# Neighbourhood attention on one Trainium2 core: the scores of two heads in one PSUM tile of two banks

## The chip, the core and the metric

One core of a Trainium2 chip runs the whole program in one launch. The metric is the device time of one execution in microseconds (us). Three executions of the kernel before took 3437.06, 3450.85 and 3451.09 us, a median of 3450.85 us.

## The reference, cut to what matters

The program is two networks in a row: a block with two attention layers and a mixture of experts, and then a two-layer block whose layers mix tokens in three ways at once (gated linear attention, a short convolution, neighbourhood attention) and end in a feed-forward part with a convolution. All arithmetic is in float32. The change sits in the neighbourhood attention of the second block. It has 512 tokens on a grid of 8 rows and 64 columns, six heads of 64 columns each, and 256 context tokens; each token attends to a window of 8 rows and 16 columns with a learnt bias, and to the whole context, under one softmax:

```python
def neighbourhood_attention(q, k, v, k_ctx, v_ctx, rpb):
    ...
    qg = grid(q.astype(jnp.float32) * (NA_DH ** -0.5))
    ...
        s_loc = jnp.einsum('bqhd,bikhd->bhqik', q_r, k_band) + jnp.transpose(bias, (0, 2, 1, 3))[None]
        s_loc = jnp.where(col_mask[None, None, :, None, :], s_loc, NEG_INF)
        s_ctx = jnp.einsum('bqhd,bchd->bhqc', q_r, kc)
        s = jnp.concatenate([s_loc.reshape(bsz, NA_HEADS, GRID_W, kh * GRID_W), s_ctx], axis=-1)
        p = jax.nn.softmax(s, axis=-1)
        ...
        o = jnp.einsum('bhqik,bikhd->bqhd', p_loc, v_band) + jnp.einsum('bhqc,bchd->bqhd', p_ctx, vc)
```

The last line adds the products of the probabilities with the values of the window and of the context.

## The kernel before, in words

The second block's main part ("latent", `lat` in the code) starts when the mixture of experts is done. It runs two layers; each is a mixer (`mixing`, line 1137) and a feed-forward part (`ffn`, line 1696). `whole` (line 1800) opens one PSUM pool, `pp`, for all of it, with four tags of two banks each: `mm`, `sc`, `tp` and `po`, which are the eight banks of PSUM. `bank` (line 163) takes a tile of one bank from it by tag. In `ffn` two more names are mapped onto the same tags: `ua` onto `mm` and `ub` onto `sc`.

In a mixer the tag `sc` is used by the gated linear attention (lines 1545, 1630 and 1688) and then by the neighbourhood attention `na` (line 1433). `na` handles the 512 queries in four blocks `b` of 128 (16 grid columns of 8 rows). For each block it loads the bias rows by DMA, adds the column mask on GpSimd (line 1450) and then goes through three pairs `j` of heads: 12 pairs in a layer, 24 in all. For one pair:

- two `sc` tiles of one bank are taken, one for each head (line 1454). Head 0 of a pair (`par` 0) has its queries and keys on partitions 0 to 63, head 1 on 64 to 127. Two matmuls for each head write its scores: 248 columns of the window (line 1460) and 256 of the context (line 1462). They are traced in the order window of both heads, context of both heads. A float32 matmul shows as two records in the trace.
- for each head VectorE adds the bias to the window's scores and takes their maximum in one instruction (line 1473), takes the context's maximum (line 1475) and joins the two (line 1476). ScalarE takes both exponentials (lines 1477 and 1478); the second reads the scores' bank last, and after it the bank is free. The sum and its reciprocal are VectorE's (lines 1479 and 1480); GpSimd scales the window's probabilities (line 1481) and VectorE the context's (line 1482).
- `pv_pair` (line 1416) transposes the probabilities on TensorE in blocks of 128 (line 1425, tag `tp`), copies them out, head 0 by VectorE and head 1 by ScalarE (line 1427), and multiplies by the values (line 1430, tag `po`). There are four such blocks for each head where `b` is 0 or 3, and five where it is 1 or 2.
- `put` splits the result into two rounded parts (`split`, lines 227 and 228) for the output projection (`add_gated`, line 1248, tag `mm`).

No order is written out by hand here: the compiler's list scheduler orders each engine's instructions ahead of time, by the order in which they were traced and by when a modelled run has their inputs and their tile's slot ready. Each engine then runs its list in that order. So instructions of one pair mix with those of the pairs before it, with the short convolution (`in_conv`), which is traced beside `na`, and with the first matmuls of the output projection, which need only the parts that are finished.

Of the kernel before, what the change touches and what calls it, by code (L numbers as in the profile page):

```python
# [11 lines left out]
F32 = mybir.dt.float32  # L12
# [7 lines left out]
PSUM = bass.MemoryType.PSUM  # L20
# [109 lines left out]
class Net:  # L130
    def __init__(self, nc, tc, ins, ctx):
        self.nc, self.tc, self.ins = nc, tc, ins
        self.side, self.banks = "left", {}
        self.cst = {}
        self.load_consts(self.pool(ctx, "consts", 1), 0)
        self.ident = self.c("ident")
        self.hp = self.pool(ctx, "hp", 1)
        self.wp = self.pool(ctx, "wp", 3)
        self.dp = self.pool(ctx, "dp", 1, space=bass.MemoryType.DRAM)
# [22 lines left out]

    def bank(self, tag, shape=(128, 512)):
        tag, bufs = self.banks.get(tag, (tag, 2))
        return self.pp.tile(list(shape), F32, name=tag, tag=tag, bufs=bufs)

    def load_consts(self, pool, g):
        self.cst[g] = pool.tile([128, CONST_N[g]], F32, name=f"cst{g}")
# [968 lines left out]
    def mixing(self, l, st, xs=None, src=None, dst=None):  # L1137


        self = copy.copy(self)  # L1140
        ins = self.ins
        lat = st == 0
        last = not lat and dst is None
        T = 512 if lat else 256
        w_in, w_out = ins["w_in_2"][l], ins["w_out_2"][l]
        es = ExitStack()
        if not lat:
            self.psum(es)
            cp = self.pool(es, "cat", 1)
        with ExitStack() as e1:  # L1150
            self.sp = self.pool(e1, "sp", 2, side="right")
            self.load_columns(self.sp, l)
            if not lat:
                self.mixer_pools(e1, l, lat)
            with ExitStack() as e2:
                xp = self.pool(e2, "xTp", 1, side="right")
                self.lp = self.pool(e2, "lp", 2, side="right")
                if lat:
                    xT = self.modulated(xp, xs, st, 0, T)
                    cp = self.pool(es, "cat", 1)  # L1160
                    self.whp = self.pool(es, "whp", 4)
                    self.mixer_pools(e1, l, lat)
                else:
                    with ExitStack() as e3:
                        xT = self.modulated(xp, self.rows_in(e3, src), st, 0, T)
                    self.wp = self.pool(e2, "bw", 2)
                    self.whp = self.pool(e2, "whp", 2)
                if lat:
                    self.parts = [cp.tile([128, 4, 8, 128], F32R, name=f"cat{a}") for a in "hl"]
                elif not last:  # L1170
                    self.parts = cp.tile([128, 8, T], F32, name="cat")
                    self.cat = self.parts.rearrange("p k (t i) -> p k t i", i=128)
                heads = self.in_heads(l, w_in, xT, T, lat, last)
                if lat:
                    finished(heads)
                else:
                    yield from heads
                gla = self.gla(l, T, lat, last)
                attention = self.in_attention(w_in, xT, T, lat, last)
                if lat:  # L1180
                    rest = itertools.chain(attention, self.in_gate(w_in, xT, T, lat))
                    together(gla, rest)
                    finished(rest)
                    self.gate()
                    rest = self.in_conv(w_in, xT, T, lat)
                    together(self.na(l), rest)
                    finished(rest)
                else:
                    yield from gla
                    yield from attention  # L1190
                    if not last:
                        yield from self.in_gate(w_in, xT, T, lat)
                        self.gate()
                        yield from self.in_conv(w_in, xT, T, lat)
            if not lat:
                if not last:
                    with ExitStack() as e2:
                        self.lp = self.pool(e2, "lp", 2)
                        yield from self.ctx_attention(T)
                for o, a in ((0, self.sfin), (192, self.nkT), (960, self.nv)):  # L1200
                    n = a.shape[1] * a.shape[2]
                    self.dma(self.ctx_out[l][:, o:o + n].rearrange("p (a b) -> p a b", a=a.shape[1]), a)
        if last:
            es.close()
            return
        if lat:
            return self.add_gated(es, self.reload, w_out, l, st)
        xs = self.rows_in(es, src)
        self.wp = self.pool(es, "bw", 2)
        self.whp = self.pool(es, "whp", 2)  # L1210
        self.lp = self.pool(es, "lp", 1)
        yield from self.add_gated(es, lambda t: xs[t], w_out, l, st, dst)
# [220 lines left out]
    def na(self, l):  # L1433
# [3 lines left out]
        for b in range(4):  # L1437
# [13 lines left out]
            for j in range(3):  # L1451
                po = self.bank("po", [128, 128])
                pms = g6("npm", [128, 2, 640])
                scs = [self.bank("sc") for _ in range(2)]
                for c in range(2):
                    for par, sc in enumerate(scs):
                        rows = slice(64 * par, 64 * par + 64)
                        q = self.nqT[rows, j, 128 * b:128 * b + 128]
                        if c == 0:
                            nc.tensor.matmul(sc[:, :248], q, self.nkT[rows, j, 8 * lo:8 * lo + 248], start=True, stop=True)  # L1460
                        else:
                            nc.tensor.matmul(sc[:, 248:504], q, self.kcT[rows, j], start=True, stop=True)  # L1462
                for par, sc in enumerate(scs):
                    pm = pms[:, par]
                    mx = self.sp.tile([128, 2], F32, name="nmx")
                    den = self.sp.tile([128, 2], F32, name="nden")
                    nm, r = self.sp.tile([128, 1], F32, name="nnm"), self.sp.tile([128, 1], F32, name="nr")
                    if o:
                        nc.gpsimd.memset(pm[:, :o], 0.0)
                    if o + 248 < 128 * ntile:  # L1470
                        nc.gpsimd.memset(pm[:, o + 248:128 * ntile], 0.0)
                    win, ctxs = pm[:, o:o + 248], pm[:, 384:640]
                    V.tensor_tensor_reduce(win, sc[:, :248], bias[:, 2 * j + par].rearrange("p c r -> p (c r)"), 1.0, NEG,
                                           ALU.add, ALU.max, accum_out=mx[:, 0:1])
                    V.tensor_reduce(mx[:, 1:2], sc[:, 248:504], axis=AX.X, op=ALU.max)
                    V.tensor_scalar(nm, mx[:, 0:1], mx[:, 1:2], -1.0, op0=ALU.max, op1=ALU.mult)
                    nc.scalar.activation(win, win, AF.Exp, bias=nm, accum_out=den[:, 0:1])
                    nc.scalar.activation(ctxs, sc[:, 248:504], AF.Exp, bias=nm, accum_out=den[:, 1:2])
                    V.tensor_tensor(r, den[:, 0:1], den[:, 1:2], op=ALU.add)
                    V.reciprocal(r, r)  # L1480
                    nc.gpsimd.tensor_scalar(win, win, r, None, op0=ALU.mult)
                    V.tensor_scalar(ctxs, ctxs, r, None, op0=ALU.mult)

                def v(i, par):
                    hv = slice(128 * j + 64 * par, 128 * j + 64 * par + 64)
                    return self.nv[:, base + i, hv] if i < ntile else self.cv[:, i - ntile, hv]

                self.pv_pair([pms[:, 0], pms[:, 1]], [128 * i for i in range(ntile)] + [384, 512], v, po)
                yield int(j % 2 == 1 or b == 3)
                self.put(lambda a: a[:, 5 + j].rearrange("p t (r c) -> p c t r", c=64)[:, 16 * b:16 * b + 16],  # L1490
                         po.rearrange("p (c t r) -> p c t r", t=4, r=2))
# [204 lines left out]
    def ffn(self, l, st, xs=None, rows=None):  # L1696

        self = copy.copy(self)
        nc, V, ins = self.nc, self.nc.vector, self.ins
        lat = st == 0  # L1700
# [11 lines left out]
        self.lp = self.pool(e1, "lp", 2, side="right")  # L1712
        tiles = []
        xT = self.modulated(xp, (tiles.append(x) or x for x in xs), st, 2, T)
        if lat:
            php = self.pool(es, "php", 1)
        lat_or = es if lat else e1
        if not lat:
            self.wp = self.pool(lat_or, "bw", 5)
# [58 lines left out]
        if not lat:  # L1778
            self.rows_out(rows, tiles)
        e1.close()  # L1780
        if not lat:
            es.close()
            return
# [79 lines left out]
```

## Time and profile before

| what | value |
|---|---|
| median of 3 executions | 3450.85 us (3437.06 to 3451.09) |
| profiled execution, its own time | 3452.61 us |
| its span (first to last instruction) | 3450.8 us |
| time around the span | 1.8 us |
| TensorE busy | 3176.0 us, 92% of the span |
| VectorE busy | 1660.2 us, 48% |
| ScalarE busy | 1165.7 us, 34% |
| GpSimd busy | 241.9 us, 7% |
| mean granted TensorE clock | 0.961 |
| neighbourhood attention, first layer | 2219.3 to 2293.0 us of the span |
| neighbourhood attention, second layer | 2928.9 to 3008.8 us |

PE is TensorE's matmul row, PEld its weight loads, DVE is VectorE, ACT ScalarE, POOL GpSimd and SP the queue that issues DMAs. Times within a trace are microseconds from the span's start. "L1460" is line 1460 of the kernel. A matmul's record begins when it starts and lasts past the start of the next one, since matmuls are pipelined; the distance from start to start is what one costs in a row of them. PEclk is the granted clock of TensorE as a share of full speed (1.00 is 2.4 GHz, 0.50 is 1.2 GHz).

### The profile page before, as it was taken

Reading aid. Unit: us, or ns where it says so; the run is one execution under the profiler, and the core shown is the slowest. Engines: PE = TensorE matmul, PEld = TensorE weight load, DVE = VectorE, ACT = ScalarE, POOL = GpSimd, SP = SyncE. Lnnn points to the kernel's source line nnn. Section 1 sums busy time; section 2 is a strip of 40 time slices with the busy share of each in tenths; the row PEclk is TensorE's granted clock in tenths of the full one; section 3 lists DMA queues with packets and bytes.
Section 4 is the critical chain, followed back from the end, with each engine's and each line's share of the span. In section 5 each row is a group of like instructions: output and inputs, shape, how many; then the busy total and the mean of one; then the engine's idle time right before and its main releaser. Section 6 shows DMA issues by size and latency. Waiting matters only on the chain. (4 is left out here: it accounts for less than half of the span.)

```text
span 3450.8 us, 47075 instructions
## 1 busy us (share of the span) xinstructions
PE 3176.0 (92%) x17636; PEld 2138.6 (62%) x17636; DVE 1660.2 (48%) x3940; ACT 1165.7 (34%) x2217; POOL 241.9 (7%) x318
## 2 busy tenths in 40 slices
PE   8996999999799979999989859999999899989998
PEld 5453345454386635756625357767888777678887
DVE  3454224223366634544524156566555556655555
ACT  3331222123255314323223144345233342443322
POOL 0000111010000011000010000130000000400000
PEclk9997999999999979999999979999999999899999
DMA  7789998999831489998899932223333232233331
GB/s 279 267 284 371 365 376 275 348 361 357 316 130 49 164 329 304 305 334 275 273 357 351 348 112 74 75 74 110 98 92 96 80 92 67 72 96 94 96 98 55
DMA packets 412976, 716.05 MB, mean 208 GB/s; under 512 B 42216, under 2 KB 266520, under 8 KB 406600
## 3 DMA queue, kind: packets, MB, share of 16 engines
q1 hardware_dynamic: 397768, 691.98, 57.8%
q0 software_dynamic: 14976, 21.02, 2.7%
q8 instruction: 141, 2.31, 0.3%
q14 instruction: 91, 0.75, 0.1%
HBM read 691.76 MB, written 37.87 MB: 211 GB/s over the span
## 5 line engine op out<-in xcount | busy, mean ns | idle before, releaser
L228 DVE TENSOR_TENSOR wl<-w,wh 128x1024 fp32r<-128x1024 f32 (+3 forms) x360 | 425.0, 1187 | 276.3 <-ACT wh L227 256.0
L227 ACT CAST wh<-w 128x1024 fp32r<-128x1024 f32 (+3 forms) x360 | 362.6, 1016 | 562.2 <-PE po L234 117.0
L795 PE MATMUL sc<-wx,xg 128*64 128x512 f32 x1492 | 434.5, 603 | 6.0 <-DMA wx<-in_moe_w_up 5.5
L232 PE MATMUL mm<-xTh,wh 128*128 128x512 f32 (+1 forms) x672 | 262.9, 391 | 1.1 <-ACT xTh L227 0.6
L234 PE MATMUL mm<-xTh,wl 128*128 128x512 f32 (+1 forms) x672 | 261.8, 390 | 1.1 <-DVE wl L228 1.1
L233 PE MATMUL mm<-xTl,wh 128*128 128x512 f32 (+1 forms) x672 | 260.0, 387 | 0.0
L795 PEld LDWEIGHTS sc<-wx,xg 128*64 128x64 f32 x1492 | 121.2, 137 | 192.6 <-issue 156.0
L732 POOL DMA_INDIRECT acc<-y,to x64 | 103.0, 1609 | 998.4 <-ACT y L809 899.6
L798 DVE TENSOR_TENSOR hid<-hid,sc 64x512 f32<-64x512 f32 x64 | 44.2, 691 | 253.4 <-ACT hid L797 252.9
L807 PE MATMUL mm<-wx,hT 128*64 128x512 f32 x580 | 153.6, 642 | 11.1 <-DVE hT L803 7.6
L232 PEld LDWEIGHTS mm<-xTh,wh 128*128 128x128 f32 x672 | 127.7, 190 | 32.2 <-issue 2.3
L232 PE MATMUL sc<-xTh,wh 128*128 128x512 f32 (+1 forms) x384 | 145.8, 380 | 0.0
L233 PE MATMUL sc<-xTl,wh 128*128 128x512 f32 (+1 forms) x384 | 145.5, 379 | 0.0
L234 PEld LDWEIGHTS mm<-xTh,wl 128*128 128x128 f32 x672 | 127.6, 190 | 28.8 <-DVE wl L228 1.5
L234 PE MATMUL sc<-xTh,wl 128*128 128x512 f32 (+1 forms) x384 | 145.4, 379 | 0.0
L233 PEld LDWEIGHTS mm<-xTl,wh 128*128 128x128 f32 x672 | 127.5, 190 | 27.0 <-issue 0.7
L232 PE MATMUL a<-xTh,wh 128*128 128x256 f32 (+2 forms) x472 | 140.1, 297 | 2.0 <-ACT wh L227 1.4
L232 PE MATMUL po<-wh,gTh 128*128 128x512 f32 x352 | 138.0, 392 | 3.8 <-DVE t2k L1727 2.8
L797 ACT ACTIVATE hid<-sc 64x512 f32<-64x512 f32 x64 | 37.7, 589 | 299.6 <-PE sc L795 299.5
L234 PE MATMUL a<-xTh,wl 128*128 128x256 f32 (+2 forms) x472 | 136.8, 290 | 1.3 <-DVE wl L228 1.2
L233 PE MATMUL po<-wl,gTh 128*128 128x512 f32 x352 | 137.2, 390 | 0.0
L234 PE MATMUL po<-wh,gTl 128*128 128x512 f32 x352 | 136.4, 390 | 0.0
(510 smaller groups left out, 6556.9 us busy)
## 6 DMA issues: line engine op xcount, KB each, us to landing
wx<-in_moe_w_up SPq DMA_DIRECT2D x192, 512.0 KB
wx<-in_moe_w_gate SPq DMA_DIRECT2D x181, 512.0 KB
wx<-in_moe_w_down SPq DMA_DIRECT2D x145, 512.0 KB
w<-in_ffn_w_up SPq DMA_DIRECT2D x264, 256.0 KB
g<-in_w_ada SPq DMA_DIRECT2D x48, 1024.0 KB
w<-in_moe_w_down SPq DMA_DIRECT2D x76, 512.0 KB
w<-in_w_in SPq DMA_DIRECT2D x70, 512.0 KB
w<-in_ffn_w_down SPq DMA_DIRECT2D x64, 512.0 KB
```

Source lines behind the costliest of these rows:

```text
L227: self.nc.scalar.copy(hi, src)
L228: self.nc.vector.tensor_tensor(lo, src, hi.bitcast(F32), op=ALU.subtract)
L232: mm(ps, ah, bh, start=start, stop=False)
L233: mm(ps, ah, bl, start=False, stop=False)
L234: mm(ps, al, bh, start=False, stop=stop)
L732: nc.gpsimd.indirect_dma_start(out=acc, out_offset=bass.IndirectOffsetOnAxis(ap=ix, axis=0), in_=y, in_offset=None, bounds_check=1023, oob ...
L795: nc.tensor.matmul(ps[r], xg[:, k], w, start=k == 0, stop=k == 7)
L797: nc.scalar.activation(hid[64:], ps[:64], AF.Silu)
L798: V.tensor_tensor(hid[64:], hid[64:], ps[64:], op=ALU.mult)
L807: nc.tensor.matmul(py[64 * h:64 * h + 64], hT[:, k], w[:, 512 * h:512 * h + 512], start=k == 0, stop=k == 3)
```

## The change

Both heads' scores of a pair go into one tile `pair` of two banks, from a pool `pairs` with a single buffer that lives for `na` alone. For this the two banks of the tag `sc` leave the pool `pp`: a pool `scp` of two banks is opened for the mixer's earlier stages and closed ahead of `na`, and another is opened for the up projection of `ffn`. `bank("sc")` takes from `scp` where there is one. PSUM stays at eight banks. The matmuls, their order in the source and everything that reads the scores stay as they were. The pools are opened with `reuse_waits="tile"`, as all of them are here: a tile that lands on a bank of a closed pool waits for the earlier users of that bank alone.

```diff
     def __init__(self, nc, tc, ins, ctx):
         ...
-        self.cst = {}
+        self.cst, self.scp = {}, None
...
     def bank(self, tag, shape=(128, 512)):
         tag, bufs = self.banks.get(tag, (tag, 2))
-        return self.pp.tile(list(shape), F32, name=tag, tag=tag, bufs=bufs)
+        pool = self.scp if tag == "sc" and self.scp else self.pp
+        return pool.tile(list(shape), F32, name=tag, tag=tag, bufs=bufs)
...
+                esc = ExitStack()
+                if lat:
+                    self.scp = self.pool(esc, "scp", 2, space=PSUM)
                 heads = self.in_heads(l, w_in, xT, T, lat, last)
...
                     rest = self.in_conv(w_in, xT, T, lat)
+                    esc.close()
+                    self.scp = None
+                    self.pairs = self.pool(esc, "pairs", 1, space=PSUM)
                     together(self.na(l), rest)
                     finished(rest)
+                    esc.close()
...
                 pms = g6("npm", [128, 2, 640])
-                scs = [self.bank("sc") for _ in range(2)]
+
+                pair = self.pairs.tile([128, 2, 512], F32, name="pair")
+                scs = [pair[:, par] for par in range(2)]
                 for c in range(2):
...
         xT = self.modulated(xp, (tiles.append(x) or x for x in xs), st, 2, T)
+        esc = ExitStack()
         if lat:
             php = self.pool(es, "php", 1)
+            self.scp = self.pool(esc, "scp", 2, space=PSUM)
...
         e1.close()
+        esc.close()
```

## Rows read from the trace of the kernel before

**Rows 1.** The page's part 1: span and busy time of each engine.

```profile
span 3450.8 us, 47075 instructions
PE 3176.0 (92%) x17636; PEld 2138.6 (62%) x17636; DVE 1660.2 (48%) x3940; ACT 1165.7 (34%) x2217; POOL 241.9 (7%) x318
```

**Rows 2.** Windows view, stretches of both layers' neighbourhood attention; columns in its first line.

```profile
core 0: us, PE busy (x) PEld busy (x) DVE busy (x) ACT busy (x) POOL busy (x), PEclk, DMA share, GB/s
2229.60:2240.00 10.40, 8.32 (x53) 5.84 (x52) 8.30 (x32) 5.32 (x19) 8.03 (x19) 0.96 0.23 46
2240.00:2264.50 24.50, 24.41 (x168) 16.38 (x166) 19.64 (x86) 14.01 (x51) 16.44 (x34) 1.00 0.16 33
2264.50:2283.00 18.50, 18.50 (x120) 12.20 (x120) 12.71 (x51) 10.62 (x38) 10.89 (x19) 1.00 0.21 43
...
2928.00:2947.20 19.20, 15.50 (x75) 9.59 (x73) 16.25 (x51) 11.44 (x32) 8.19 (x13) 1.00 0.40 101
2947.20:2964.30 17.10, 17.09 (x65) 11.22 (x65) 8.44 (x39) 5.48 (x19) 6.60 (x18) 0.50 0.20 42
```

**Rows 3.** Timeline of PE, first layer, one head by itself (start, us, operation).

```profile
2264.59 0.68 PE L1460 MATMUL sc<-nkT,nqT 64*128 64x248 f32 x2
2265.12 0.59 PE L1462 MATMUL sc<-arena,nqT 64*128 64x256 f32 x2
2265.64 0.43 PE L1430 MATMUL po<-g2k,cv 128*64 128x128 f32 x2
```

**Rows 4.** Timeline of PE, first layer, pair 1: both heads in turn.

```profile
2229.64 1.10 PE L1460 MATMUL sc<-nkT,nqT 64*128 64x248 f32 x4
2230.57 0.60 PE L1462 MATMUL sc<-arena,nqT 64*128 64x256 f32 x4
2231.10 1.09 PE L1425 MATMUL tp<-cst,npm 128*128 128x128 f32 x8
```

**Rows 5.** Source view of L1460: what ended TensorE's idle time before it.

```profile
  ACT npm L1478: 10.5, 17
```

**Rows 6.** Timelines of DVE and ACT, first layer, pair 1.

```profile
2231.20 0.42 DVE L1473 CUSTOM_DVE_ANT_0 npm<-sc,bias 128x248 f32<-128x248 f32 x1 [1.37 <-PE sc L1462]
...
2232.79 0.68 DVE L1427 COPY g2k<-tp 128x512 f32<-128x512 f32 x1
...
2234.21 0.47 ACT L1478 ACTIVATE npm<-sc,nnm 128x256 f32<-128x256 f32 x1
```

**Rows 7.** Timeline of PE, first layer: first scores of pairs 0 and 11, last product.

```profile
2219.29 0.68 PE L1460 MATMUL sc<-nkT,nqT 64*128 64x248 f32 x2
...
2279.31 0.68 PE L1460 MATMUL sc<-nkT,nqT 64*128 64x248 f32 x2
...
2292.26 0.70 PE L1430 MATMUL po<-g2k,cv 128*64 128x128 f32 x7
```

**Rows 8.** The same, second layer: first scores of pairs 0, 1, 4, 6, 11, last product.

```profile
2928.91 0.68 PE L1460 MATMUL sc<-nkT,nqT 64*128 64x248 f32 x2
...
2937.80 0.68 PE L1460 MATMUL sc<-nkT,nqT 64*128 64x248 f32 x2
...
2950.78 1.19 PE L1460 MATMUL sc<-nkT,nqT 64*128 64x248 f32 x2
...
2967.82 0.68 PE L1460 MATMUL sc<-nkT,nqT 64*128 64x248 f32 x2
...
2995.17 0.68 PE L1460 MATMUL sc<-nkT,nqT 64*128 64x248 f32 x2
...
3008.10 0.70 PE L1430 MATMUL po<-g2k,cv 128*64 128x128 f32 x7
```

**Rows 9.** Tile view of sc, 2100 to 2400 us: last column is first and last start.

```profile
L232 PE MATMUL sc<-xTh,wh x48: 277/281/562, 2347.7 to 2399.7; 128*128 128x256 f32 x32, 128*128 128x512 f32 x16
...
L1478 ACT ACTIVATE npm<-sc,nnm x24: 452/454/486, 2227.6 to 2286.5; 128x256 f32<-128x256 f32 x24
```

**Rows 10.** Timeline of POOL, first layer, pair 11: the scaling of the second head.

```profile
2287.65 0.92 POOL L1481 TENSOR_SCALAR npm<-npm,nr 128x248 f32<-128x248 f32 x1 [2.31 <-ACT cath L227]
```

## The prediction, made before the change was run

> **What bounds the kernel now.** I read the page's engine shares first: TensorE is busy for 92% of the span, every other engine for under half [rows 1]. A share of the whole says little on a change to two stretches, so I went to the windows of the neighbourhood attention. They show three regimes [rows 2]. Early in a layer TensorE is busy for 8.32 of 10.40 us: it waits for softmaxes. From 2240 us it is busy without a gap (24.41 of 24.50, 18.50 of 18.50) at full clock, while VectorE and ScalarE have room (12.71 and 10.62 of 18.50). And in the second layer there are 17.1 us at a granted clock of 0.50, the 1.2 GHz level; ahead of it TensorE had been busy for 15.50 of 19.20 us. So the middle of the stage is TensorE's, and what it does there counts in full.
>
> The timeline shows what it does with the scores. A head issued by itself takes 0.53 us for the window and 0.52 for the context, start to start [rows 3]; two heads are 2.1 us. In pair 1 of the first layer both heads were issued in turn, and there the context scores of both took 0.53 us [rows 4]: one head on each half of the rows costs what one head costs. That is the only pair of the 24 issued so; in the others the heads stand apart; as I read it, because their two banks came free at different times.
>
> **The change, part by part.**
>
> Removed: the separate slots. Both banks now come free together, so the four score matmuls become ready together and in source order, heads in turn. A pair's scores then cost 2 x 0.53 = 1.05 us, for 2.1: 1.05 saved. The nearest row for less is the window half of that pair [rows 4], 0.93 us from 2229.64 to 2230.57; with it a pair costs 1.46 and saves 0.64. I take 1.05, since the context half shows what side by side gives when it holds throughout.
>
> Added: a wait. The next pair's first score waits for the second head's last exponential, where today each head waits for its own. Those single waits are 10.5 us over 17 times in both layers [rows 5]. Behind the waiting matmul in TensorE's list stand transposes and products of the pair before; they wait with it unless the scheduler puts them ahead, as it may, since they are older. Softmaxes of two pairs no longer overlap. So the stage gets a cycle of one pair, C, and three things bound it:
> - the round trip of the buffer. Of a pair issued together [rows 4, 6] the scores end at 2231.10, VectorE starts at 2231.20, the second head's exponential ends at 2234.68: 3.58 us, with a 0.68 us copy of the pair before inside. With 1.05 for scores and another 0.1 to the next start it is 4.73; without the copy 4.05.
> - TensorE's own work. The 18.50 us window without a gap holds the scores of six heads (counted in the timeline), three pairs: 6.17 each, so 5.12 after the saving. Pairs with four blocks rather than five have less.
> - VectorE's work: 12.71 / 3 = 4.24 a pair.
>
> C lies between 4.05 and 6.17 (nothing gained). I take 5.1: the larger of the first two, as each has the other's work as cover.
>
> A layer is then: first pair to second, unchanged, 10.35 and 8.89 us [rows 4, 7, 8], because the first pair waits for no earlier one; ten cycles; and a tail from the last pair's scores. That tail is 13.65 us now, 2279.31 to 2292.26 + 0.70 = 2292.96 [rows 7], with more than one pair's products left over. In lockstep only one pair is left: 4.7 for scores and softmax, and then, of the 5.31 us from the start of the last scaling [rows 7, 10] in which two pairs are finished, about 4.5 with the reciprocal: 9.2 (bounds 8 and 10.7).
>
> | layer | before | after, C = 5.1 | difference |
> |---|---|---|---|
> | first | 2292.96 - 2219.29 = 73.67 | 10.35 + 51 + 9.2 = 70.55 | -3.1 |
> | second | 3008.80 - 2928.91 = 79.89 | 8.89 + 51 + 9.2 = 69.09 | -10.8 |
>
> That is -13.9 us with no stretch at 1.2 GHz. I don't believe in none: TensorE has more pauses in lockstep, and both layers begin with the 80% that went ahead of the slow stretch. That stretch held pairs 4 and 5, 17.04 us from 2950.78 to 2967.82 [rows 8], 8.52 each; one such stretch costs 2 x (8.52 - 5.1) = 6.8. Sum: -13.9 + 6.8 = -7.1 us.
>
> Edits at nothing: the pools. No instruction is added. At a change of pool a tile waits only for its bank's last users; the first scores of a layer may wait for one bank more, under 1 us of the first 10, which other work fills (0 to 1 us a layer, no gain possible). In the feed-forward part the first `ub` tile starts at 2347.7, 61 us after the last exponential at 2286.5 [rows 9]; that gap is its cover. No DMA moves on SP or on POOL's queue; the loads of bias rows wait for SBUF tiles, not for scores. If the next thing is late, it is these biases (GpSimd, 16.44 of 24.50 us busy [rows 2]).
>
> The profiled execution took 3452.61 us, 1.8 over the median of 3450.85; the sum is made on its rows and taken from the median: **3450.85 - 7.1 = 3443.7 us**. About 0.5% (17.3 us: below 3433.6 or above 3468.1) is what a measurement of this kernel can tell from no change.
>
> **Rivals.**
> - *All of it arrives.* C = 4.6, near the round trip, and no slow stretch: 10.35 + 46 + 9.2 = 65.55 and 64.09, -8.1 and -15.8: 3426.9 us. For it: VectorE and ScalarE have room. Against: 5.12 of TensorE's work where there are five blocks. Chance 0.18.
> - *The reads set the pace.* VectorE's 4.24 us a pair fall outside the scores' 1.05 and two hops, C = 5.4: 73.6 and 72.1, -0.1 and -7.8, and +6.2 for a slow stretch: 3449.2 us, nothing to be seen. For it: with one buffer no scores lie ready while VectorE finishes a pair. Against: it has copies and scalings to do then. Chance 0.18. The Trainium skill (TensorEngine Tiling (Array Packing), PSUM Bottleneck) says that packing the array speeds TensorE but not the reading of PSUM, which may become the bound; before the change the trace does not show it, with VectorE at 12.71 of 18.50 us.
> - *Slower: the clock.* With a pause in each cycle TensorE stays at 1.2 GHz in much of the stage, and a pair costs 8.52. Each such pair costs 3.4: four use up the 13.9, nine make the kernel slower by over 0.5%, and with 12 of 24 it is +41.0 - 13.9 = +27.1: 3478 us. For it: two pairs ran so already, after 81% busy. Against: the first layer had the same start and stayed at 0.96 to 1.00 [rows 2]. Chance 0.18.
> - *It doesn't do what it says.* Older transposes cut between the heads, the scores stay at 2.1 and the lockstep comes on top: C = 6.15, 81.05 and 79.59, +7.4 and -0.3: 3458 us. Chance 0.09.
>
> **How the numbers follow.** My case has 0.37, with its own range 3434 to 3455 (no slow stretch to two, C from 4.9 to 5.4). The range reaches to the full gain and into the slow clock, 3424 to 3474, and leaves out some 0.15. Faster by over 0.5%: most of the first rival and the edge of mine, 0.22. Slower: most of the clock's, 0.17. Within: 0.61.
>
> **What would show it.** Right: score records in groups of four (L1460 and L1462), some 1.05 us a pair at full clock; TensorE's waits for L1478 above 10.5 us in all; pauses of TensorE in windows that had none; the last products closer to the last scores, 9 for 13.65 us; cycles near 5.1. The forecast is wrong if cycles are under 4.7 or over 5.6, if more than four pairs run at 1.2 GHz, or if time moves outside the two stretches, which no step here allows for.

## The result and the profile after: slower by 1.4%

| | before | after |
|---|---|---|
| median, us | 3450.97 (3437.06 to 3451.15, 4 runs) | 3495.82 (3492.13 to 3498.39, 4 runs) |
| profiled execution, us | 3452.61 | 3498.39 |

The ratio is 1.0136 with a 95% interval of 1.0117 to 1.0154. The forecast was 3443.7 us with a range up to 3474: wrong in sign, and outside the range.

Page, part 1, of the kernel after, to be held against [rows 1]:

```profile
span 3496.6 us, 47049 instructions
PE 3173.6 (91%) x17636; PEld 2133.6 (61%) x17636; DVE 1663.9 (48%) x3940; ACT 1166.8 (33%) x2217; POOL 242.0 (7%) x318
```

No engine has much more work (TensorE 3173.6 us for 3176.0, VectorE 1663.9 for 1660.2); the span is 45.8 us longer, and that is waiting. The windows view of the kernel after, over the first layer's stretches of [rows 2] with the rest of the stage, and a stretch of its second layer (us, busy time of each engine, PEclk, DMA):

```profile
2229.60:2240.00 10.40, 6.54 (x41) 4.31 (x42) 5.44 (x20) 3.28 (x12) 6.96 (x12) 0.84 0.11 24
2240.00:2264.50 24.50, 18.32 (x119) 12.42 (x120) 16.39 (x62) 10.63 (x37) 13.14 (x32) 0.78 0.17 32
2264.50:2283.00 18.50, 14.33 (x101) 9.43 (x97) 11.06 (x43) 7.90 (x28) 7.43 (x14) 0.83 0.22 43
2283.00:2319.00 36.00, 27.48 (x164) 17.21 (x164) 19.07 (x67) 16.11 (x47) 10.03 (x17) 0.81 0.06 20
...
2975.00:3005.00 30.00, 21.60 (x146) 14.59 (x143) 17.20 (x67) 11.66 (x41) 15.29 (x38) 0.84 0.13 27
```

Where TensorE was busy for 24.41 of 24.50 and 18.50 of 18.50 us it now is for 18.32 and 14.33, and so are the others: everybody waits. The clock in these stretches is 0.78 to 0.84.

First scores of pairs 0 and 11 and the last product, timeline of PE, both layers, to be held against [rows 7, 8]:

```profile
2220.49 0.69 PE L1470 MATMUL pair<-nkT,nqT 64*128 64x248 f32 x4
...
2305.89 0.69 PE L1470 MATMUL pair<-nkT,nqT 64*128 64x248 f32 x4
...
2315.43 1.26 PE L1438 MATMUL po<-g2k,cv 128*64 128x128 f32 x7
...
2956.51 0.69 PE L1470 MATMUL pair<-nkT,nqT 64*128 64x248 f32 x4
...
3045.50 0.69 PE L1470 MATMUL pair<-nkT,nqT 64*128 64x248 f32 x4
...
3055.54 0.70 PE L1438 MATMUL po<-g2k,cv 128*64 128x128 f32 x7
```

| layer | span before | forecast | span after | mean cycle, before / forecast / after |
|---|---|---|---|---|
| first | 73.67 | 70.55 | 2316.69 - 2220.49 = 96.20 | 4.97 / 5.1 / 7.49 |
| second | 79.89 | 69.09 | 3056.24 - 2956.51 = 99.73 | 5.74 / 5.1 / 7.90 |

(A mean cycle here and below is from the first scores of pair 1 to those of pair 11, over ten.) The two layers hold 42.4 of the 45.8 us that the profiled executions differ by; the other 3.4 lie around them.

What the change was meant to do, it does. Timeline of PE of the kernel after, pair 4 and the start of pair 5:

```profile
2251.79 0.65 PE L1433 MATMUL tp<-cst,npm 128*128 128x128 f32 x4 [2.04 <-POOL npm L1491]
2252.38 0.69 PE L1470 MATMUL pair<-nkT,nqT 64*128 64x248 f32 x4
2252.90 0.60 PE L1472 MATMUL pair<-arena,nqT 64*128 64x256 f32 x4
...
2258.55 0.69 PE L1470 MATMUL pair<-nkT,nqT 64*128 64x248 f32 x4 [1.00 <-ACT npm L1488]
```

Both heads are issued in turn in all 24 pairs, in 22 of them with nothing in between, and at full clock a pair's scores cost 0.52 for the window and 0.53 for the context, as [rows 4] had promised. Then comes what no step had allowed for. Timelines of PE (the last of its scores) and DVE, pair 3 of the kernel after, to be held against [rows 6]:

```profile
2246.56 0.83 PE L1472 MATMUL pair<-arena,nqT 64*128 64x256 f32 x4
...
2247.44 0.42 DVE L1483 CUSTOM_DVE_ANT_0 npm<-pair,bias 128x248 f32<-128x248 f32 x1 [1.07 <-PE pair L1472]
...
2248.24 0.21 DVE L1486 TENSOR_SCALAR nnm<-nmx 128x1 f32<-128x1 f32 x1
2249.76 0.16 DVE L1489 TENSOR_TENSOR nr<-nden 128x1 f32<-128x1 f32 x1 [1.31 <-ACT npm L1488]
2249.84 0.42 DVE L1483 CUSTOM_DVE_ANT_0 npm<-pair,bias 128x248 f32<-128x248 f32 x1
```

and of ACT:

```profile
2249.11 0.45 ACT L1488 ACTIVATE npm<-pair,nnm 128x256 f32<-128x256 f32 x1
...
2251.15 0.50 ACT L1487 ACTIVATE npm<-npm,nnm 128x248 f32<-128x248 f32 x1 [0.99 <-DVE nnm L1486]
```

The second head's scores lie ready from 2247.39 on (2246.56 + 0.83). VectorE is idle for 1.31 us, until the first head's last exponential is done (2249.11 + 0.45 = 2249.56), does that head's sum, and only then takes the second head's maximum; then ScalarE idles for 0.99. The two heads go through VectorE and ScalarE one behind the other. So it is in all 24 pairs: 2.80 and 2.72 us on the mean (first and second layer, ten pairs each) from one head's maximum to the other's. That distance by itself is not new: in the kernel before, whose heads are scored apart, it was 2.36 and 2.80. What is new is what waits for it. Before, the next pair's first scores started 1.39 and 1.34 us ahead of the end of a pair's last exponential; now they start 0.82 and 0.97 us behind it.

The waits of the whole kernel, source views of L1489, L1433 and L1470 (the last answers [rows 5]):

```profile
  ACT npm L1488: 43.3, 42
...
  POOL npm L1491: 62.5, 42
...
  ACT npm L1488: 14.7, 11
```

and of the same sum and transposes in the kernel before (L1479, L1425):

```profile
  ACT npm L1478: 5.3, 8
...
  POOL npm L1481: 1.5, 5
```

The sum (L1489) waits 43.3 us over 42 times; before it was 5.3 over 8. The transposes (L1433) wait 62.5 us for GpSimd's scaling, for 1.5 over 5 before: probabilities come later, and nothing is left to cover it.

### The profile page after: what moved, and what is told of

It reads as the page before. It is cut to its first block, busy times and chain, and to the rows that moved or that the text cites. A ratio compares the mean times of both kernels' runs of the same rounds, so it can differ in the third digit from the quotient of the medians.

```text
span 3496.6 us, 47049 instructions
## 1 busy us (share of the span) xinstructions
PE 3173.6 (91%) x17636; PEld 2133.6 (61%) x17636; DVE 1663.9 (48%) x3940; ACT 1166.8 (33%) x2217; POOL 242.0 (7%) x318
```

## The experiments

Four theories stood at the start. A: the one tile of two banks ties the heads, so that the second head's read by VectorE stands behind the first head's read by ScalarE. B: the joint release of a single buffer is dear by itself. C: the clock is a cause of its own. D: the pools.

**Undoing the order, or the tile.** The first two runs keep one buffer. In one, both heads' maxima are traced ahead of both exponentials:

```diff
                 for par, sc in enumerate(scs):
...
                     V.tensor_scalar(nm, mx[:, 0:1], mx[:, 1:2], -1.0, op0=ALU.max, op1=ALU.mult)
+                    heads.append((sc, win, ctxs, nm, den, r))
+                for sc, win, ctxs, nm, den, r in heads:
                     nc.scalar.activation(win, win, AF.Exp, bias=nm, accum_out=den[:, 0:1])
```

> The changed kernel with the source order of one pair's softmax altered: the maxima of both heads are traced ahead of the exponentials of either. Tile, pools, joint release and all arithmetic as in the changed kernel. Theory A (one tile of two banks orders the heads: the second head's VectorE reads stand behind the first head's ScalarE read in every pair, which makes a cycle of 7.5 to 7.9 us of one of about 5): the cycle falls to 4.7 to 5.6 us and the time to 3435 to 3460 us. Theory B (the single buffer, so the joint release, is what costs): cycles stay above 6.5 and the time above 3475 us. Theory C (TensorE's clock at 1.2 GHz is a cause of its own, set off by any pause): between the two, 3460 to 3475, with a granted clock of 0.8 in the stage.

Measured: 3455.75 us, ratio 1.0014 (1.0000 to 1.0029), cycles 6.15 and 5.92. Some 40 of the 45 us are back. In the other the source order stays, and the tile is two:

```diff
-                pair = self.pairs.tile([128, 2, 512], F32, name="pair")
-                scs = [pair[:, par] for par in range(2)]
+                scs = [self.pairs.tile([128, 512], F32, name=f"pair{par}", tag=f"pair{par}") for par in range(2)]
...
                     nc.scalar.activation(ctxs, sc[:, 248:504], AF.Exp, bias=nm, accum_out=den[:, 1:2])
+                    if par:
+                        keep = self.sp.tile([128, 1], F32, name="nkeep")
+                        nc.scalar.copy(keep, scs[0][:, :1])
```

> The changed kernel with two tiles of one bank each in place of the tile of two banks; the source order of the softmax is the changed kernel's. A copy of one column from head 0's bank, traced after the second head's last exponential, keeps head 0's bank held until the pair is done, so the release stays joint. 24 small ScalarE copies are added (about 0.2 us each). Theory A (ordering through the shared tile): the second head's maxima move ahead of the first head's sum without any change of source order, cycles of 4.7 to 5.8 us, 3440 to 3465 us. Theory B (joint release): 3475 us or more, as in the changed kernel.

Measured: 3459.13 us, 1.0030 (1.0013 to 1.0048), cycles 6.17 and 5.91. The copy held the release together in the first layer; in most of the second it ran right behind the first head's exponential, so there the release was not joint. The second head's maximum now came ahead of the first head's last exponential in all twelve pairs of the first layer and in eight of the second, although the source order was the changed kernel's: it is the tile that orders the heads.

**Parts that should cost little.** The pools alone (two tiles of the old kind, from a pool of the stage), and, in the kernel before, the changed kernel's order of the heads alone:

```diff
-                pair = self.pairs.tile([128, 2, 512], F32, name="pair")
-                scs = [pair[:, par] for par in range(2)]
+                scs = [self.pairs.tile([128, 512], F32, name="sc", tag="sc", bufs=2) for _ in range(2)]
```

> The changed kernel's pools per stage, but the neighbourhood attention takes its scores as before, in two tiles of one bank with two buffers under one tag, from the stage's pool. Theories A, B and C: the pools cost nothing, 3440 to 3458 us, within 0.3% of the kernel before. Rival D (the pools' closing and opening costs): 3475 us or more.

```diff
+                    with self.tc.issue_after(summed) if par else nullcontext():
                         V.tensor_tensor_reduce(win, sc[:, :248], bias[:, 2 * j + par].rearrange("p c r -> p (c r)"), 1.0, NEG,
...
-                    V.tensor_tensor(r, den[:, 0:1], den[:, 1:2], op=ALU.add)
+                    summed = V.tensor_tensor(r, den[:, 0:1], den[:, 1:2], op=ALU.add).ins
```

> The kernel before, with one order added on VectorE: the second head's first maximum is issued behind the first head's sum. Two separate banks and two buffers stay. Theory A: the order alone costs, but two buffers hide part of it, since the next pair's first head can be scored meanwhile: 3455 to 3485 us. Theory B: with the buffers separate nothing much happens, 3445 to 3457 us.

Measured: the pools 3457.94 us, 1.0025 (1.0009 to 1.0041), cycles 5.51 and 5.64; the order in the kernel before 3454.22, 1.0007 (0.9991 to 1.0023), cycles 5.28 and 5.26. So the order alone costs nothing that can be seen where each head's bank is released by itself. The run with the pools alone is 0.25% slower, more than the 0 to 2 us of the forecast; where, the runs don't show.

**Is it a wait of its own?** In the kernel after, the first head's sum stands ahead of the second maximum and hides what that one waits for. The next run moves sum, reciprocal and scaling of both heads behind the second head's exponentials:

```diff
                     nc.scalar.activation(ctxs, sc[:, 248:504], AF.Exp, bias=nm, accum_out=den[:, 1:2])
+                    heads.append((win, ctxs, den, r))
+                for win, ctxs, den, r in heads:
                     V.tensor_tensor(r, den[:, 0:1], den[:, 1:2], op=ALU.add)
```

> The changed kernel with one tile of two banks, but the first head's sum, reciprocal and scaling are issued after the second head's maxima and exponentials. VectorE is then free, and no longer stands behind the first head's sum, when the second head's scores are there. Theory A1 (the shared tile itself ties the second head's maximum to the first head's exponential): the second maximum now shows a wait for ScalarE of its own in most of the 24 pairs, the cycles stay near 7.5 us and the time at 3480 to 3498 us. Rival A2 (only the order in which VectorE's list was written cost the time): the second maximum follows the first without a wait for ScalarE, cycles near 6.0, 3448 to 3463 us.

Measured: 3473.49 us, 1.0065 (1.0037 to 1.0093), cycles 6.79 and 6.77: between the two forecasts. Source view of the maximum in this run (L1484; L1489 is its last exponential):

```profile
  ACT npm L1489: 23.2, 21
  PE pair L1472: 13.0, 15
```

The wait is there, 23.2 us of it, and it is ScalarE's. The built instruction list names it as well, in all 24 pairs. Here, for one pair of this run (first and second head of a pair), and for the two tiles of the run of 3446.04 us below:

```
L1484 ISA npm_19725,nmx_19731<-pair_19726,bias_19646 128x248 [waits PE_49]
L1484 ISA npm_19725,nmx_19742<-pair_19726,bias_19646 128x248 [waits Activation_49]

L1486 ISA npm_19838,nmx_19845<-pair0_19839,bias_19655 128x248 [waits PE_49]
L1486 ISA npm_19838,nmx_19860<-pair1_19840,bias_19655 128x248 [waits PE_49]
```

So the wait is written into the program where two engines read one PSUM tile, though each head has its bank. Sharing a tile in SBUF does not bring it: `npm`, which takes both heads' probabilities, is one tile in the lower two lines too, and there the second maximum waits for TensorE alone. Half of the loss is gone when only the sum steps aside; neither theory had that. The trace says where it went: the second maximum still comes 2.69 us behind the first (2.76 in the kernel after, both layers together), so the tie is there in full. Of the 0.91 us a cycle that are back, 0.58 lie behind the pair: the next scores start 0.31 us after the last exponential, for 0.89.

**Two buffers.** The same tile with two buffers (the banks come from `mm` and `po`, which have one each in these two stages), with the changed kernel's order, and with both maxima first:

```diff
...
-                    self.pairs = self.pool(esc, "pairs", 1, space=PSUM)
+                    self.pairs = self.pool(esc, "pairs", 2, space=PSUM)
...
```

> The changed kernel with two buffers of the two-bank tile in the two neighbourhood stages; the four banks come from one bank less for the projections and one less for the heads' outputs there, elsewhere each has two as before. The order of the two heads through the tile stays. Theory A with B (the order costs because nothing else can run in it: the next pair's scores wait for the one tile): cycles of 5.0 to 5.8 us, 3438 to 3460 us. Rival (the order costs by itself, on VectorE): cycles stay above 6.8, 3475 us or more. Rival (the banks taken from the projections and outputs cost as much as the second buffer returns): cycles between 5.8 and 6.8 with TensorE waiting for those.

> Both maxima ahead of both exponentials (as in the first run of the study) and two buffers of the two-bank tile as in the run beside it. If the single buffer set the 6.0 us cycle that was left there: cycles of 4.9 to 5.4 us, 3430 to 3445 us, faster than both kernels. If the clock, the ScalarE and VectorE copies or the GpSimd scaling set it: cycles of 5.6 to 6.1, 3450 to 3462 us.

Measured: 3446.97 us, 0.9994 (0.9979 to 1.0009), cycles 5.48 and 5.50; and 3441.64 us, 0.9975 (0.9957 to 0.9993), cycles 5.45 and 5.24. With a second buffer the tied heads cost nothing that can be seen. The loss needs both, the order and the single buffer.

> The changed kernel with two tiles of one bank in the place of one tile of two, each released by its own head's reads (the run with the joint release kept gave 3459.13). If the joint release by itself costs nothing: within 4 us of that run, 3454 to 3463 us. If it costs: the first head's bank is free some 1.5 us sooner in a pair, 3436 to 3452 us.

This run is the one with two tiles, without the copy that joined their releases: 3456.68 us, 1.0028 (1.0012 to 1.0044), cycles 5.30 and 5.64. By their times the joint release costs nothing against it (1.0030 for 1.0028). But the run with the copy kept the release joint in the first layer alone, and there its cycle is 6.17 us for 5.30, in a profiled execution of 3467.20 us, 8 us over that run's median. So these two runs leave the question open; the clean pair below answers it, with a joint release in every pair at 0.9987.

**The forecast's own cycle.** What was left, 5.9 to 6.2 with one buffer, was still above 5.1. In those runs VectorE took the maxima of both heads before the first head's `nm`, so that ScalarE started late. The next run puts the second head's maximum behind it, on the two tiles with the copy:

```diff
+                    with self.tc.issue_after(lowest) if par else nullcontext():
                         V.tensor_tensor_reduce(win, sc[:, :248], bias[:, 2 * j + par].rearrange("p c r -> p (c r)"), 1.0, NEG,
...
-                    V.tensor_scalar(nm, mx[:, 0:1], mx[:, 1:2], -1.0, op0=ALU.max, op1=ALU.mult)
+                    lowest = V.tensor_scalar(nm, mx[:, 0:1], mx[:, 1:2], -1.0, op0=ALU.max, op1=ALU.mult).ins
```

> The run with two tiles of one bank and the joint release kept (3459.13, cycles 6.17 and 5.91), with one thing more: the second head's maximum is issued behind the first head's nm on VectorE, so that the first head's exponentials start while VectorE does the second head's maxima, as the forecast had it. If the round trip of scores, reads and release sets the cycle: from the start of the scores to the release 4.6 to 5.0 us for 5.4 to 5.8, cycles of 5.1 to 5.5, 3438 to 3452 us. If the copies of the transposes, the GpSimd scaling or the clock set it: the hold gets shorter and the gap behind it longer, cycles stay at 5.8 to 6.2, 3453 to 3463 us.

Measured: 3450.49 us, 1.0004 (0.9988 to 1.0020), cycles 5.14 and 5.47. But the copy ran early in every pair, so the release was not joint, and the run doesn't test what it should. Beside it ran three with four banks: two tiles with two buffers each, the run of 3441.64 again, and that one with the new order.

> Two tiles of one bank with two buffers each (four banks, as in the run of 3441.64 with two buffers of the two-bank tile), so that nothing ties the heads and each bank is released by itself. If the two more banks are what made that run faster than the kernel before: 3434 to 3446 us here too. If it was the joint release with both maxima first (groups of four, fewer switches between stages): 3447 to 3460 us.

> The kernel of 3441.64 us (both maxima first, two buffers of the two-bank tile) again with more rounds, beside its two relatives. If it is faster than both kernels: 3436 to 3446 us and a ratio to the kernel before with its upper end below 1. If that was chance: a ratio that holds 1.

> The kernel beside it, with the second head's maximum issued behind the first head's nm on VectorE. Through the shared tile the first head's exponentials still have to stand behind the second head's maxima, so the order should bring little: within 5 us of the kernel beside it. If the tile ties only a later maximum to an earlier exponential and not the other way: the first head's exponentials run beside the second head's maxima, and the time is 3430 to 3438 us.

Measured: 3441.82 (0.9983; 0.9969 to 0.9997), 3442.45 (0.9981; 0.9967 to 0.9994) and 3433.97 us (0.9958; 0.9942 to 0.9975), the last with cycles of 5.18 and 5.07: the fastest kernel here, ahead of both. Its main expectation missed; the other one had the time, but by a tie in one direction only. The timeline of ACT shows what happens instead:

```profile
2242.95 0.50 ACT L1495 ACTIVATE npm<-npm,nnm 128x248 f32<-128x248 f32 x1 [2.55 <-DVE nr L1498]
...
2243.61 0.48 ACT L1496 ACTIVATE npm<-pair,nnm 128x256 f32<-128x256 f32 x1
```

The tie works in this direction too: the context's exponential starts when VectorE's last read of the second head's bank ends (2243.16 + 0.41 = 2243.57), and in the instruction list it waits for VectorE. But the window's exponential reads `npm`, not the tile, and now goes ahead.

**The clean pair.** Two runs differ in one order alone. Both have two tiles, the copy fixed behind the second head's last exponential (`issue_after`), the four score products fixed in turn, one buffer. One has the second maximum behind the first head's `nm`, the other behind the first head's sum.

> Two tiles of one bank, with groups of four and the joint release now fixed by order (ScalarE's copy of one column stands behind the second head's last exponential), one buffer each, and the second head's maximum behind the first head's nm: the cycle as the forecast described it, with some 0.2 us of copy on top. If the forecast's bounds for an independent pair hold: 4.6 to 4.9 us from scores to release, cycles of 5.2 to 5.6, 3441 to 3455 us. If joint release with one buffer is dear by itself: cycles of 5.8 or more, 3457 us or more.

> The same kernel but for one order: the second head's maximum stands behind the first head's sum on VectorE, as it does in the changed kernel, though no tile is shared. If that order together with the joint release of a single buffer is all there is to the loss: cycles of 7.4 to 8.1 us and 3485 to 3502 us, like the changed kernel. If the shared tile costs in some other way too: below 3480 us.

Measured: 3446.04 us, 0.9987 (0.9973 to 1.0001), cycles 5.51 and 5.37; and 3487.97 us, 1.0102 (1.0082 to 1.0122), cycles 7.16 and 7.31. Source views of the sum (L1496) and of the transposes (L1433) in the slower one:

```profile
  ACT npm L1491: 24.2, 22
  ACT nkeep L1495: 17.8, 22
...
  POOL npm L1498: 54.3, 45
```

These are the changed kernel's waits, 42.0 us at the sums and 54.3 at the transposes, with no shared tile. In the faster one the transposes' is 18.7 over 19:

```profile
  POOL npm L1498: 18.7, 19
```

Its DVE timeline, pair 2:

```profile
2233.90 0.41 DVE L1486 CUSTOM_DVE_ANT_0 npm<-pair,bias 128x248 f32<-128x248 f32 x1 [0.23 <-PE pair L1474]
...
2234.70 0.21 DVE L1489 TENSOR_SCALAR nnm<-nmx 128x1 f32<-128x1 f32 x1
2234.83 0.40 DVE L1486 CUSTOM_DVE_ANT_0 npm<-pair,bias 128x248 f32<-128x248 f32 x1
...
2235.16 0.42 DVE L1488 TENSOR_REDUCE nmx<-pair 128x1 f32<-128x256 f32 x1
```

and its ACT timeline:

```profile
2235.01 0.50 ACT L1490 ACTIVATE npm<-npm,nnm 128x248 f32<-128x248 f32 x1 [2.02 <-DVE nnm L1489]
...
2235.51 0.45 ACT L1491 ACTIVATE npm<-pair,nnm 128x256 f32<-128x256 f32 x1
```

0.93 us lie between the heads' maxima, for 2.40 in the pair of the kernel after shown above, and VectorE and ScalarE read the two heads' banks at the same time (2235.16 to 2235.58 and from 2235.51).

| second maximum behind the first head's exponentials | released bank by bank | one buffer, joint release | two buffers of the pair |
|---|---|---|---|
| yes | 1.0007 (kernel before, ordered) | 1.0136 (the change); 1.0102 (by hand) | 0.9994 |
| no | 1 (kernel before) | 0.9987 | 0.9958 |

(The left column has the pools of the kernel before. With the changed pools, each bank released by itself and no order laid on, the runs gave 1.0025 and 1.0028.)

## Why the prediction was wrong

**The step that failed** is the first of the three things that bound C: the round trip of the buffer, 4.05 to 4.73 us. It was read from a pair whose heads had a tile each [rows 4, 6], where VectorE works on the second head while ScalarE does the first, and it was taken over to one tile. From a pair's first scores to the end of its last exponential the kernel after takes 6.68 us on the mean in the first layer and 6.93 in the second. In the run of 3446.04 us, with the joint release and without the tie, it is 4.81 and 4.93, and 4.96 and 5.07 with the copy that ends the hold there: just above those bounds. The change does not only free two banks together: it makes two reads of one tile out of reads that had nothing to do with each other. Cut into its parts, the cycle shows where the time went (means of both layers' twenty cycles, us):

| part of the cycle | the kernel after | order by hand (3487.97) | without the order (3446.04) |
|---|---|---|---|
| the scores, first start to last end | 1.64 | 1.43 | 1.35 |
| to the first head's maximum | 0.11 | 0.09 | 0.08 |
| to the second head's maximum | 2.76 | 2.71 | 1.12 |
| to the end of its last exponential | 2.29 | 2.19 | 2.32 |
| to the next pair's scores | 0.89 | 0.81 | 0.57 |
| cycle | 7.69 | 7.23 | 5.44 |

Of 2.25 us a cycle 1.64 lie between the two heads' maxima. The two layers miss their forecast by 56.3 us together, and 51.9 of these are the cycles (ten of 7.49 - 5.1 and ten of 7.90 - 5.1); the rest is in the tails and in the second layer's first pair to second, 10.02 us for 8.89.

**The rest of C.** In the first layer C = 5.1 was no less than the mean cycle before, 4.97: all that the forecast gained there came from the tail. I took the larger of the bounds, "as each has the other's work as cover". It was not full cover: behind the last exponential TensorE starts the next scores 0.82 and 0.97 us later in the kernel after, 0.70 and 0.44 (copy of 0.15 us included) in the run without the tie. So that run's C is 5.51 and 5.37, for 5.1. Its tails are 9.21 and 9.16 us where the forecast had 9.2; in the kernel after they are 10.80 and 10.74, with the second head later. That run's time, 3446.04, lies near the forecast of 3443.7, but in part by luck: its cycles are longer than forecast, its first pair to second shorter (8.27 us in both layers for 10.35 and 8.89), and its two layers take 143.7 us where the forecast, slow stretch included, had 146.4.

**Removed.** Right: the heads in turn in 24 of 24 pairs, 1.05 us a pair at full clock.

**The clock.** This rival had the sign, and more than four pairs do run at 1.2 GHz: of the twenty pairs that a mean cycle is taken from, nine have score groups longer than 1.7 us (2.05 where all of it is at 1.2 GHz, 1.12 at full clock). These nine cycles are 7.74 us on the mean. Of the other eleven, four take 9.13 to 10.14 us (those that end the two middle blocks of queries), and the remaining seven 6.66. So cycles with slow scores are the longer ones, and the clock may well have a share in the loss: the scores, on which it acts directly, grew by 0.29 us a cycle in the table above. But the rival's condition, that a pause in each cycle is enough, does not hold: in the run of 3446.04 us TensorE pauses in 16 of 20 cycles as well, and 15 of the 20 are at full clock from end to end, for 5 of 20 in the kernel after. And the five cycles at full clock are 6.41 us on the mean, for 5.41 of the fifteen, with 2.67 us between the two heads' maxima for 1.19: the order costs time where the clock never fell. How the rest divides between the order and the clock is open.

**The reads set the pace.** Its C of 5.4 (3449.2 us) is what one buffer gives without the tie. The Trainium skill (TensorEngine Tiling (Array Packing), PSUM Bottleneck) warns that reading PSUM may become the bound once the array is packed. The trace agrees: of 5.51 us a cycle (first layer of that run) 4.81 go from the first scores to the end of the last exponential, 1.12 of them scores at full clock. What cost the most here is the order of the reads.

The Trainium skill (PSUM — Partial Sum Buffer, PSUM bank collisions raise a hardware error) asks that accesses of two engines to the same bank and quarter of the partitions be kept apart, reads by VectorE and ScalarE among them. The heads' banks differ, so by that rule no wait was due here. The run of 3446.04 us agrees, where ScalarE reads the first head's bank and VectorE the second's side by side for as long as 0.37 us:

```profile
2980.53 0.45 ACT L1491 ACTIVATE npm<-pair,nnm 128x256 f32<-128x256 f32 x1
2980.61 0.42 DVE L1488 TENSOR_REDUCE nmx<-pair 128x1 f32<-128x256 f32 x1
```

In the kernel after no such pair of reads overlaps at all: the program guards the two banks as one tile.

**The pools.** Costed at 0 to 1 us a layer; 3457.94 for 3447.97 us in the run with the pools alone. Under-sized, place open. The 7.9 us between the change and the order laid on by hand stay open too.

## What to carry to other kernels

Before two buffers are joined into one PSUM tile, list who reads each half, and on which engine: a wait may appear between reads that shared nothing, and it shows in the instruction list before anything runs. With one buffer, what lies between a tile's first write and its last read is paid in every cycle, so the order of the reads inside it is worth more than the engine time that grouping saves (1.05 us a pair saved, 2.0 and 2.5 lost: 7.49 - 5.51 and 7.90 - 5.37). Here each half of the remedy alone gave back nearly all, and order and a second buffer together made the change a gain: 3433.97 us. How much of that gain is the tile's is not shown, since two tiles of one bank with two buffers each gave 3441.82 without the order.

## What the runs showed that was not expected

A wait can stand in the profile under another instruction's name. L1483, the second maximum, shows no idle time for ScalarE in the kernel after; the 43.3 us stand at the sum ahead of it, and only in the run that moves the sum away does a wait for ScalarE, 23.2 us of it, appear at the maximum.

A mean over unlike cycles can hide what a low clock costs. In the kernel after, the nine cycles with score groups at half clock and the other eleven have nearly the same mean (7.74 and 7.66 us), because four of the eleven, of 9.13 to 10.14 us, stand at the end of a block. Without these four it is 7.74 for 6.66.
